# A two-layer transformer with routed experts on one Trainium2 core: the first expert blocks straight behind the choice of experts

## The chip, the core and the metric

The kernel runs on one core of a Trainium2 chip. The metric is the device time of one execution in microseconds (us). The engines are PE (TensorE, matmuls; its weight loads are listed as PEld), DVE (VectorE), ACT (ScalarE), POOL (GpSimd) and SP (SyncE, which issues nearly all DMAs).

## The reference

A sequence of 256 tokens of width 1024 passes two layers. Layer 0 mixes with a gated MLP, layer 1 with causal attention; behind each mixer stands a mixture of experts, and all vectors are modulated by a conditioning vector `c` (`ada`). The part at issue is `moe`, computed once in each layer:

```python
scores = jax.nn.sigmoid((xt @ w_router).astype(jnp.float32))
choice = scores + e_bias
...
choice = jnp.where(emask, choice, NEG_INF)      # the best 4 of 8 groups
_, eidx = lax.top_k(choice, TOP_K)              # 8 of 64 experts for each token
w = jnp.take_along_axis(scores, eidx, axis=1)
w = w / jnp.sum(w, axis=-1, keepdims=True) * ROUTED_SCALE
routed = grouped_experts(xt, eidx, w, w_gate, w_up, w_down)
shared = swiglu(xt, ws_gate, ws_up, ws_down)
return (routed + shared)
```

Each expert is `(silu(x @ wg) * (x @ wu)) @ wd` with 1024 x 256, 1024 x 256 and 256 x 1024 weights in float32, so 3 MB; all 64 are read in each layer, 192 MB. The shared expert has the same size and takes all tokens.

## The kernel before, in words

**Weights.** Every weight comes in loads of 1 MB (`load`, L255), issued by SP in one fixed order into 14 buffers ("w" tiles): 9 of a pool for the whole program and 5 of the stage's own. An expert is three loads, written here as e.0 (gate and up, first half of the contraction), e.1 (second half) and e.2 (down). A load is issued when the tile that used its buffer before has been read for the last time; SP waits there, and all later loads wait behind it.

**The stage of experts** (`moe`, L669) does this in each layer. Experts 0 and 1 and the shared expert are loaded before anything is known of the tokens. The router's logits are made, the scores (`sc`), the choice, and from the counts the rank of every expert: PE, DVE and PE again end in the tile `order` (L845), from which SP reads the number of each further expert before it loads it (`get_w`, L905). So expert weights beyond 0 and 1 cannot be asked for earlier than `order`. Ranks, not expert numbers, have a fixed number of token slots (`CAPS`); `_plan` (L70) cuts the slots, in the order of the list `ORDER`, into 55 blocks of 64, b0 to b54: one expert with 64 slots, or two with 32 each. `_loads` (L115) plans in the same order which buffer pool each load takes.

**Between the choice and b0** PE and DVE work through what the code writes there, each engine in the order of the program: sums of the conditioning vector that are still open (in layer 0, L852, 16 matmuls `wk<-w,cs`; in layer 1 the second gate is finished by `flush` in L889), the shared expert's gate and up product (`shared_up`, L769: 32 matmuls of 128x256, in pieces of 4, 12, 4 and 12, the 4 of `SH1` before the choice), the slots (`psu`, `slotU`), the weights of the slots (`wsel`, `GT`, `gu`), and the scaling of the gate into the shared expert's down weights (`gates`, L762). Then come the slots' one-hot matrix (`prep`, L920), 32 gather matmuls for the first four blocks (`gather`, L951) and the share of each slot (`share`, L932).

**A block** (`run`, L1085): `gate_up` (16 or 32 matmuls), `act` (ACT silu, DVE product with the slot's share), then `down` of the block before, the transposition of the new block, `place`, the scatter of the block before that, and one fourth of the gather for the next group of four blocks. The shared expert's `shared_down` (8 matmuls of 128x512) stands ahead of block `SHARED_AT`, b3. Its three buffers carry expert weights afterwards, as do those of the open sums. `e.0` and `e.1` are free when `gate_up` has read them, `e.2` when `down` has, which stands behind the next block's `gate_up`.

In the trace an fp32 matmul is recorded as two, so `x24` are 12 matmuls. All operations are recorded at line 200, so rows are told apart by tiles: `wk<-b,w 128*128` is `shared_up`, `wk<-w,b` `gate_up`, `wk<-w,ht` `down`, `acc<-w,s` `shared_down`, `wk<-s,b 128x256` the gather, `wk<-half,w` the end of an open sum.

Of the kernel before, what the change touches and what calls it, by code (L numbers as in the profile page):

```python
# [8 lines left out]
F32 = mybir.dt.float32  # L9
F32R = mybir.dt.float32r  # L10
# [6 lines left out]
P = 128  # L17
# [43 lines left out]

SH = -1
ORDER = [
# [3 lines left out]
]  # L67


# [34 lines left out]
BLOCKS, UNITS, SHARED_AT = _plan()  # L104


PAD = (224, 416)


SLOTS = 14  # L110
NOWN = 5
SH1 = 4


def _loads(l):  # L115

    last = {}
    for b, blk in enumerate(BLOCKS):  # L120
        for s in blk:
            if s:
                last[s[0]] = b
    items = [("e", k) for k in list(range(STATIC)) + [k for k in ORDER if k >= STATIC]]
    for i in reversed(range(NA if l == 0 else 0)):
        items.insert(AMONG[i][0], ("A", i, AMONG[i][1]))

    free = [(-9, 0)] * NOWN + [(-1, 1)] * 2 + [(2 * SHARED_AT - 1, 1)] + [(-2, 1)] * (SLOTS - NOWN - 3)
    own = []
    for x in items:  # L130
        for q in range(3 if x[0] == "e" else 1):
            free.sort()
            own.append(free[0][1] == 0)
            free[0] = (2 * last[x[1]] + (0 if q < 2 else 3) if x[0] == "e" else 2 * x[2] + 4, free[0][1])
    return items, own
# [50 lines left out]
def tile_model(ctx: ExitStack, tc: tile.TileContext, A: dict, out: bass.AP):  # L186
# [101 lines left out]
    def tb(name, rows=P):  # L288
        a, n = _TAB[name]
        return tab[0:rows, a:a + n]  # L290
# [25 lines left out]
    G.affine_select(tris, onesb[0:NE, 0:NE], [[1, NE]], ALU.is_gt, 0.0, base=0, channel_multiplier=-1)  # L316
    mhalf = cst.tile([P, 2], F32, name="mhalf")
    G.memset(mhalf, -0.5)
    pidxb = cst.tile([NE, 1], BF16, name="pidxb")
    G.iota(pidxb, [[0, 1]], base=0, channel_multiplier=1, allow_small_or_imprecise_dtypes=True)  # L320
    cs = cst.tile([P, KT], F32, name="cs")
# [347 lines left out]
    def moe(l, own, rw, first, rest):  # L669

        def om(shape, dt=F32, tag="sm", bufs=5):
            return own.tile(list(shape), dt, tag=tag, name=nm(tag), bufs=bufs)
# [54 lines left out]
        logits(4)  # L727
        pr = along([r[:, tt:tt + 1] for tt in range(2)])
        rb = h1((P, 256))
        S.copy(rb, pr)  # L730
        acc = accs()
        for q, x in enumerate(xs):
            T.matmul(acc[q], ident, x, start=True, stop=True, skip_group_check=True)
# [2 lines left out]
        lg = om([P, 2, NE])  # L736
        for tt in range(2):
            V.scalar_tensor_tensor(lg[:, tt, :], pl[tt], r[:, tt:tt + 1], cb, ALU.mult, ALU.add)
        for k, eng, b in ((0, V, pr), (4, G, rb)):
            eng.tensor_tensor(hT[:, k:k + 4, :], xT[:, k:k + 4, :], b.unsqueeze(1).to_broadcast([P, 4, 256]), ALU.mult)  # L740


        sc = om([P, 2, NE])
        S.activation(sc, lg, AF.Tanh, scale=0.5)
        for k in range(KT):
            S.activation(hT[:, k, :], hT[:, k, :], AF.Identity, bias=sh2[:, k:k + 1], scale=sc2[:, k:k + 1])
        for q in range(4):
# [1 line left out]
            t = s2((P, 512))  # L749
            S.activation(t, xs[q], AF.Copy, scale=r[:, q // 2:q // 2 + 1])  # L750
            G.tensor_tensor(pieces(rl)[q], t, pieces(rh)[q], ALU.subtract)
        V.tensor_scalar(sc, sc, 0.5, 0.5, ALU.mult, ALU.add)

        wsh = first[0]
        hid = s2((P, 2, 256))
# [6 lines left out]
        def gates():  # L762

            for q in range(2):
                S.copy(gq[64 * q:64 * q + 64, :], g2[l][64 * q:64 * q + 64, 512 * q:512 * q + 512])
            for k, eng in enumerate((G, V)):
                eng.tensor_tensor(wsh[2][:, k, :], wsh[2][:, k, :], g2[l], ALU.mult)

        def shared_up(n):  # L769
            for f, q, k in todo[:n]:  # L770
                if q == k == 0:
                    psh.append(wk((P, 2, 256)))
                T.matmul(psh[f][:, q, :], wsh[k // 4][:, k % 4, q * 256 + f * P:q * 256 + (f + 1) * P], hT[:, k, :],
                         start=(k == 0), stop=(k == KT - 1))
            del todo[:n]
# [50 lines left out]
            T.matmul(pn[:, 0:NE], c64b, sel[:, tt, :], start=(tt == 0), stop=(tt == 1))  # L826
        for tt in range(2):
            T.matmul(pn[:, NE:NE + 1], sel[:, tt, :], c64b[:, 0:1], start=(tt == 0), stop=(tt == 1))
        slot = om([P, 2, NE], BF16, tag="slot", bufs=1)
        V.tensor_tensor(slot, pc, sel, ALU.mult)  # L830
        keyr = om([NE, NE])
# [20 lines left out]
        while sums:  # L852
            rest(1)
            pump(T, S)
        shared_up(16 - SH1)
        slotT = om([NE, 256], BF16, tag="slotT", bufs=1)
        V.tensor_copy(slotT, pst)
        puf = om([NE, NU], tag="puf", bufs=1)
        V.tensor_scalar(puf, tb("rk", NE), rank, None, ALU.is_equal)
        pub = om([NE, NU], BF16, tag="pub", bufs=1)  # L860
        V.tensor_copy(pub, puf)

        wsel = om([P, 2, NE])
        wsum = om([P, 2], tag="t1", bufs=8)
        for tt in range(2):
            V.scalar_tensor_tensor(wsel[:, tt, :], cr[:, tt, :], -2.5e38, sc[:, tt, :], ALU.is_lt, ALU.mult,
                                   accum_out=wsum[:, tt:tt + 1])
        wrec = om([P, 2], tag="t1", bufs=8)
        V.reciprocal(wrec, wsum)
        for tt in range(2):  # L870
            V.tensor_scalar(wsel[:, tt, :], wsel[:, tt, :], wrec[:, tt:tt + 1], 2.5, ALU.mult, ALU.mult)
        ready = all(f.dst is None for f in active)
        if ready:
            gates()
        psu = wk((P, 2, NU))
        for tt in range(2):
            T.matmul(psu[:, tt, :], slotT[:, tt * P:(tt + 1) * P], pub, start=True, stop=True)
        settle(1)
        close()
        shared_up(4)  # L880
        pgt = wk((NE, 256))
        for tt in range(2):
            T.transpose(pgt[:, tt * P:(tt + 1) * P], wsel[:, tt, :], ident)
        settle()
        close()
        GT = om([NE, 256], tag="GT", bufs=1)
        S.copy(GT, pgt)
# [3 lines left out]
        pgu = wk((P, 2, NU))
        for tt in range(2):
            T.matmul(pgu[:, tt, :], GT[:, tt * P:(tt + 1) * P], puf, start=True, stop=True)
        gu = om([P, 2, NU, 2], F32R, tag="gu", bufs=1)
        V.tensor_copy(gu[:, :, :, 0], pgu)
        V.tensor_tensor(gu[:, :, :, 1], pgu, gu[:, :, :, 0], ALU.subtract)
        shared_up(12)
        slotU = om([P, 2, NU], tag="slotU", bufs=1)
        V.tensor_tensor(slotU, psu, tb("base").unsqueeze(1).to_broadcast([P, 2, NU]), ALU.subtract)

# [135 lines left out]

        ng = NU // 8
        prep(0)
        shared_act(0)
        shared_act(1)  # L1040
        for c in range(4):
            gather(0, c)
        share(0)
        prep(1)

        found = []

# [37 lines left out]
        def run():  # L1085
            ht, ys, sts, segs = {}, {}, {}, {}
            i0, _ = _TAB["idx"]

            def finish(b):

                return down(ht.pop(b), segs.pop(b))

            for b in range(nblk + 2):
                g, j = divmod(b, 4)

                late = b >= nblk - 1
                if b == SHARED_AT:
                    shared_down()
                if b == nblk - 1:
                    ys[b - 1] = halves(finish(b - 1))  # L1100
                if b < nblk:
                    segs[b] = segs_of(b)
                    hg = groups[g][3]
                    pg = gate_up(lambda k, a0, a1: hg[:, k, j * 64 + a0:j * 64 + a1], segs[b])
                    hd = act(pg, groups[g][2][64:128, j // 2, j % 2:j % 2 + 1])
                if late:
                    if b < nblk:
                        scatter(sts.pop(b - 2), ys.pop(b - 2))
                        ht[b] = flip(hd)
                        scatter(sts.pop(b - 1), ys.pop(b - 1))  # L1110
                    if b == nblk:
                        y = finish(b - 1)
                    if b == nblk + 1:
                        warm(10)
                        scatter(sts.pop(b - 2), ys.pop(b - 2))
                elif b:
                    y = finish(b - 1)
                if b < nblk:
                    if not late:
                        ht[b] = flip(hd)  # L1120
                    pp = place(groups[g][1][:, 2 * j:2 * j + 2, :].rearrange("e u i -> e (u i)"))
                    if b >= 2 and not late:
                        scatter(sts.pop(b - 2), ys.pop(b - 2))
                    if j == 1 and g + 1 < ng:
                        share(g + 1)
                    if g + 1 < ng:
                        gather(g + 1, j)
                if b == nblk or b >= 1 and not late:
                    ys[b - 1] = halves(y)
                if b < nblk:  # L1130
                    sts[b] = placed(pp, tab[:, i0 + b:i0 + b + 1])
                    if j == 3 and g + 2 < ng:
# [638 lines left out]
```

## Time and profile before

| | |
|---|---|
| median of 3 runs | 1399.44 us (1397.13 to 1403.96) |
| the profiled execution, its own time | 1401.17 us |
| its span, first to last instruction | 1399.4 us, mean granted clock of TensorE 0.978 |
| PE / DVE / ACT / POOL busy | 96% / 54% / 32% / 4% |
| read from HBM | 513.75 MB, 368 GB/s over the span |
| DMA queue of SP (q1) | 513.77 MB, 90.5% of 16 engines' span |
| PE waiting for expert weights (`PE wk <- DMA w<-in_wexp_dram`) | 20.2 us in 14 waits |

The span is the profiled execution between its first and its last instruction. The page's 40 slices (35 us each) show two long stretches in which the DMA engines are full at 425 or 426 GB/s: the expert stages, from slice 8 to 20 and from 28 to the end. PE is shown as busy for 96% of the span, but the ends of pipelined matmuls are modelled, so that a full PE row does not say that PE is what the program waits for.

### The profile page before, as it was taken

What the parts mean: (1) busy time and instruction counts of PE and PEld (TensorE: products, weight loads), DVE (VectorE), ACT (ScalarE), POOL (GpSimd) and SP (SyncE); (2) the same over time, 40 slices, a digit from 0 to 9 for tenths busy, and PEclk for the clock granted to TensorE, in tenths of its full rate; (3) what the DMA queues carried; (4) which work ended last, traced back from release to release, by engine and by line L of the source; (5) the groups of instructions that cost most, each with busy time, mean ns of one, the idle gap of its engine ahead of it and who ended that gap; (6) DMA issues with size and microseconds to landing.
All of it is one profiled execution on the core that took longest, in us unless ns stands there. A gap on an engine that the chain in (4) does not pass through costs nothing. (4 is left out here: it accounts for less than half of the span.)

```text
span 1399.4 us, 26932 instructions
## 1 busy us (share of the span) xinstructions
PE 1339.6 (96%) x10954; PEld 886.3 (63%) x10954; DVE 758.0 (54%) x1408; ACT 452.2 (32%) x921; POOL 57.6 (4%) x70
## 2 busy tenths in 40 slices
PE   8999999899999999998989999999999999999997
PEld 6899776555655555564649886765565556555553
DVE  3599945444455444444458866554444444444444
ACT  4444424122232222222344543322223222232222
POOL 1000002000000000000010320200000000000000
PEclk8899999999999999999999989999999999999999
DMA  9999876699999999999998855669999999999995
GB/s 387 332 342 360 313 267 240 262 402 425 426 426 425 426 373 426 426 426 426 426 408 318 295 205 216 271 230 394 418 426 426 426 426 425 426 426 426 426 426 218
DMA packets 91128, 516.60 MB, mean 369 GB/s; under 512 B 8308, under 2 KB 8436, under 8 KB 34934
## 3 DMA queue, kind: packets, MB, share of 16 engines
q1 hardware_dynamic: 90420, 513.77, 90.5%
q8 instruction: 88, 1.44, 0.4%
q10 hardware_dynamic: 580, 1.06, 0.2%
q14 instruction: 40, 0.33, 0.1%
HBM read 513.75 MB, written 1.05 MB: 368 GB/s over the span
## 5 line engine op out<-in xcount | busy, mean ns | idle before, releaser
L200 PE MATMUL wk<-w,b 128*32 128x256 f32 (+1 forms) x4928 | 415.6, 387 | 20.2 <-DMA w<-in_wexp_dram 20.2
L200 PEld LDWEIGHTS wk<-w,b 128*32 128x32 f32 (+1 forms) x4928 | 236.0, 123 | 166.2 <-DMA w<-in_wexp_dram 22.4
L200 DVE TENSOR_TENSOR s<-s,s 64x512 fp32r<-64x512 f32 x220 | 151.1, 687 | 123.5 <-ACT s L200 121.8
L200 PE MATMUL wk<-w,ht 128*32 128x512 f32 (+1 forms) x1232 | 211.5, 599 | 0.0
L200 ACT ACTIVATE b<-wk,adaT,sc 128x256 f32<-128x256 f32 x112 | 63.3, 565 | 285.6 <-DVE b L200 285.6
L200 DVE TENSOR_SCALAR b<-wk,sc,adaT 128x256 f32<-128x256 f32 x112 | 60.9, 544 | 156.0 <-PE wk L200 155.8
L200 PE MATMUL wk<-s,b 128*128 128x256 f32 (+2 forms) x1024 | 140.8, 287 | 0.0
L200 ACT CAST s<-s 64x512 fp32r<-64x512 f32 x220 | 134.3, 611 | 15.5 <-DVE s L200 12.8
L200 PEld LDWEIGHTS wk<-s,b 128*128 128x128 f32 (+1 forms) x1024 | 130.9, 187 | 10.3 <-issue 1.1
L200 PE MATMUL acc<-s,h 128*128 128x512 f32 x440 | 132.7, 423 | 0.4 <-DVEq L1147 0.4
L200 DVE TENSOR_TENSOR s<-wk,g 128x512 f32<-128x512 f32 x110 | 76.1, 692 | 89.2 <-PE wk L200 88.9
L200 PEld LDWEIGHTS wk<-w,ht 128*32 128x32 f32 (+1 forms) x1232 | 53.3, 121 | 99.7 <-issue 91.6
L200 ACT ACTIVATE h<-wk 64x256 f32<-64x256 f32 (+1 forms) x114 | 42.9, 376 | 211.7 <-PE wk L200 211.6
L200 DVE SCALAR_TENSOR_TENSOR h<-wk,ws,h 64x256 f32<-64x256 f32 x110 | 54.0, 491 | 98.1 <-ACT h L200 97.3
L200 DVE TENSOR_TENSOR scr<-w,scr 128x1024 fp32r<-128x1024 f32 x80 | 97.5, 1232 | 10.2 <-ACT scr L200 10.1
L200 ACT CAST scr<-w 128x1024 fp32r<-128x1024 f32 x80 | 83.1, 1047 | 51.7 <-PE wk L200 33.2
L200 PEld LDWEIGHTS acc<-s,h 128*128 128x128 f32 x440 | 74.4, 189 | 24.0 <-DVEq L1147 1.1
L200 ACT COPY ht<-wk 128x128 f32<-128x128 f32 x110 | 29.3, 266 | 185.4 <-PE wk L200 185.4
L200 PEld LDWEIGHTS wk<-ident,h 64*128 64x128 f32 (+1 forms) x226 | 22.5, 137 | 94.8 <-DVE h L200 93.9
L200 PE MATMUL wk<-hh,scr 128*128 128x256 f32 x576 | 73.0, 286 | 1.3 <-POOL hh L200 1.3
L200 PEld LDWEIGHTS wk<-hh,scr 128*128 128x128 f32 x576 | 70.5, 194 | 1.7 <-POOL hh L200 1.7
L200 PE MATMUL acc<-scr,hh 128*128 128x256 f32 x384 | 52.9, 299 | 4.8 <-DVE hh L200 4.5
(245 smaller groups left out, 1238.8 us busy)
## 6 DMA issues: line engine op xcount, KB each, us to landing
w<-in_wexp_dram SPq DMA_DIRECT2D x384, 1024.0 KB, 16.6
w<-in_wada_dram SPq DMA_DIRECT2D x48, 1024.0 KB, 7.6
w<-in_win_dram SPq DMA_DIRECT2D x16, 1024.0 KB, 7.5
w<-in_wqkvo_dram SPq DMA_DIRECT2D x16, 1024.0 KB, 7.8
w<-in_wkva_dram SPq DMA_DIRECT2D x8, 1024.0 KB, 6.8
w<-in_wout_dram SPq DMA_DIRECT2D x8, 1024.0 KB, 7.5
w<-in_wsh_dram SPq DMA_DIRECT2D x6, 1024.0 KB, 6.6
xt<-in_x_dram SPq DMA_DIRECT2D x1, 1024.0 KB, 6.4
```

What stands on the lines that cost most here:

```text
L200: r = f(*a, **k)
```

## The change

Nothing is added to or taken from what is computed. (1) `sc` is finished on ACT by a second activation, straight behind the tanh, in place of a DVE operation behind DVE's half of `hT`; the copy `rb` stands behind them, and POOL's half of `hT` is cut in two. (2) Before the choice 8 matmuls of `shared_up` are issued instead of 4, 2 more between the count and the rank, 6 behind the open sums; the other 16, the second half, move into the loop, behind the `act` of b3 (`UP_AT`). (3) `prep(0)` and the gather come directly behind `psu` and `slotU`; six matmuls whose result nobody reads (`warm(6)`) stand ahead of them. The weights of the slots are computed during the gather; `share(0)`, `prep(1)`, the gates and the end of the open sums move behind `gate_up` of b0. (4) `ORDER` changes, `shared_down` moves to b4, and the planned release of the shared expert's buffers follows. The number of blocks stays 55.

```diff
-    0, 63, 21, -1, 52, 56, 1, 32, 7, 46, 43, 36, 45, 6, 25, 23, 44, 15, 20, 26, 27, 30, 51, 8, 11, 50, 28, 41,
+    0, 63, 21, 52, 56, 43, -1, 59, 7, 46, 1, 36, 45, 25, 23, 44, 15, 20, 26, 27, 30, 51, 8, 11, 9, 50, 28, 41,
...
-SH1 = 4
+SH1 = 8
+
+UP_AT = 3
...
-    free = [(-9, 0)] * NOWN + [(-1, 1)] * 2 + [(2 * SHARED_AT - 1, 1)] + [(-2, 1)] * (SLOTS - NOWN - 3)
+    free = [(-9, 0)] * NOWN + [(2 * UP_AT - 1, 1)] * 2 + [(2 * SHARED_AT - 1, 1)] + [(-2, 1)] * (SLOTS - NOWN - 3)
...
-        S.copy(rb, pr)
...
-        for k, eng, b in ((0, V, pr), (4, G, rb)):
-            eng.tensor_tensor(hT[:, k:k + 4, :], xT[:, k:k + 4, :], b.unsqueeze(1).to_broadcast([P, 4, 256]), ALU.mult)
...
         S.activation(sc, lg, AF.Tanh, scale=0.5)
+        S.activation(sc, sc, AF.Identity, bias=phalf, scale=0.5)
+        S.copy(rb, pr)
+        for k, n, eng, b in ((0, 4, V, pr), (4, 2, G, rb), (6, 2, G, rb)):
+            eng.tensor_tensor(hT[:, k:k + n, :], xT[:, k:k + n, :], b.unsqueeze(1).to_broadcast([P, n, 256]), ALU.mult)
...
-        V.tensor_scalar(sc, sc, 0.5, 0.5, ALU.mult, ALU.add)
...
+        shared_up(2)
         slot = om([P, 2, NE], BF16, tag="slot", bufs=1)
...
-        shared_up(16 - SH1)
+        shared_up(16 - SH1 - 2)
...
-        V.tensor_copy(pub, puf)
+        V.tensor_scalar(pub, tb("rk", NE), rank, None, ALU.is_equal)
+        psu = wk((P, 2, NU))
+        for tt in range(2):
+            T.matmul(psu[:, tt, :], slotT[:, tt * P:(tt + 1) * P], pub, start=True, stop=True)
...
-        ready = all(f.dst is None for f in active)
-        if ready:
-            gates()
-        psu = wk((P, 2, NU))
-        for tt in range(2):
-            T.matmul(psu[:, tt, :], slotT[:, tt * P:(tt + 1) * P], pub, start=True, stop=True)
-        settle(1)
-        close()
-        shared_up(4)
-        pgt = wk((NE, 256))
...
-        if not ready:
-            flush(lambda f: f.dst is not None)
-            gates()
...
-        shared_up(12)
...
         prep(0)
+        warm(6)
+        wrec = om([P, 2], tag="t1", bufs=8)
...
         shared_act(0)
-        shared_act(1)
+        pgt = wk((NE, 256))
         for c in range(4):
             gather(0, c)
-        share(0)
-        prep(1)
+            if c == 1:
+                for tt in range(2):
+                    T.transpose(pgt[:, tt * P:(tt + 1) * P], wsel[:, tt, :], ident)
+                GT = om([NE, 256], tag="GT", bufs=1)
+                S.copy(GT, pgt)
+        pgu = wk((P, 2, NU))
...
+        def late_gates():
+            flush()
+            gates()
...
+                    if b == 0:
+                        share(0)
+                        prep(1)
                     hd = act(pg, groups[g][2][64:128, j // 2, j % 2:j % 2 + 1])
+                    if b == 0:
+                        late_gates()
+                    if b == UP_AT:
+                        shared_up(16)
+                        shared_act(1)
```

What stands on PE in layer 0 between `order` and the end of b0, before the change (`cs` marks the open sums, `pub` the slots, `half` the end of a sum, `sm` and `puf` the slots' weights, `s,b` the gather, `gu` the share, `w_1985` weights of expert 0):

```order
L200 MATMUL wk_2187<-w_345,cs 32x512 x4
L200 MATMUL wk_2115<-b_299_2080,w_335 128x256 x4
L200 MATMUL wk_2115<-b_299_2080,w_333 128x256 x4
...
L200 MATMUL wk_2235<-pub_2221,slotT_2217 128x112
L200 MATMUL wk_2238<-half_80,w_345 128x2 x4
L200 MATMUL wk_2244<-b_299_2080,w_333 128x256 x4
L200 MATMUL wk_2249<-ident,sm_2223 64x128 x2
L200 MATMUL wk_2254<-puf_2219,GT_2252 128x112 x2
...
L200 MATMUL wk_2285<-s_345_2274,b_279_1997 128x256
...
L200 MATMUL wk_2329<-gu_2257,s_345_2274 128x8 x4
L200 MATMUL wk_2346<-w_1985,b_347_2278 64x256 x8
L200 MATMUL wk_2366<-ident,h_362_2363 128x64 x2
```

The same place in the changed kernel:

```order
L202 MATMUL wk_2196<-w_347,cs 32x512 x4
L202 MATMUL wk_2118<-b_299_2081,w_335 128x256 x2
L202 MATMUL wk_2118<-b_299_2081,w_337 128x256 x4
...
L202 MATMUL wk_2224<-pub_2222,slotT_2220 128x112
L202 MATMUL wk_2238<-onesf,ident 128x128 x6
L202 MATMUL wk_2255<-s_337_2233,b_279_1999 128x256
...
L202 MATMUL wk_2254<-ident,sm_2227 64x128 x2
...
L202 MATMUL wk_2303<-puf_2249,GT_2279 128x112 x2
L202 MATMUL wk_2309<-w_1987,b_339_2237 64x256 x8
...
L202 MATMUL wk_2326<-gu_2306,s_337_2233 128x8 x4
L202 MATMUL wk_2346<-half_80,w_347 128x2 x4
L202 MATMUL wk_2356<-ident,h_360_2343 128x64 x2
```

Six matmuls of `shared_up` are left in front of the gather, the share and the end of the open sum stand behind `gate_up` of b0, and the slots' weights lie inside the gather.

On PE in layer 0 around b3 (`w_2613` and `w_2595` are first loads of an expert of b3, `w_337` and `w_339` the shared expert's down weights), before:

```order
L200 MATMUL wk_2574<-s_358_2341,b_280_1998 128x256
L200 LDWEIGHTS pidxb
L200 MATMUL wk_2593<-ohjb_2514,pidxb 1x96
L200 MATMUL acc_2072<-w_337,s_306_2113 128x512
...
L200 MATMUL wk_2634<-w_2613,b_347_2278 32x256
...
L200 MATMUL wk_2670<-w_2529,ht_2565 64x512 x4
L200 MATMUL wk_2677<-ident,h_423_2667 128x64 x2
```

and now:

```order
L202 MATMUL wk_2564<-s_357_2338,b_280_2000 128x256
L202 LDWEIGHTS pidxb
L202 MATMUL wk_2583<-ohjb_2504,pidxb 1x96
L202 MATMUL wk_2616<-w_2595,b_339_2237 32x256
...
L202 MATMUL wk_2652<-b_299_2081,w_335 128x256 x4
L202 MATMUL wk_2652<-b_299_2081,w_337 128x256 x4
...
L202 MATMUL wk_2672<-w_2519,ht_2555 64x512 x4
...
L202 MATMUL acc_2073<-w_339,s_306_2116 128x512
...
L202 MATMUL wk_2753<-w_2732,b_359_2342 32x256
```

The 16 late matmuls of `shared_up` stand between `gate_up` of b3 and `down` of b2, and `shared_down` ahead of b4's `gate_up` instead of b3's.

What each load waits for also moves, as the buffers are handed on in another order. In layer 0 the first loads behind the choice, in the names of ranks, were released like this before: 63.0 to 63.2 by the open sums, 21.0 by the end of the last open sum, 21.1 and 21.2 by the shared expert's gate and up weights, 52.0 and 52.1 by b1's `gate_up`. Now 21.0 waits for the end of that sum behind b0's `gate_up`, 21.1 and 21.2 for b1's `gate_up`; 52.2 for b2's `gate_up`, 56.1 for `down` behind it, 43.0 to 59.0 for b3's `gate_up`, 59.1 and 59.2 for the late half of `shared_up`, 7.0 for `shared_down`. In layer 1 four loads (63.0 to 21.0) find free buffers in both; then 21.1 waits for the end of the second gate's sum, 21.2 and 52.0 before for the shared expert's gate and up weights, now for b1's `gate_up`; now 56.0 and 56.1 wait for b2's, 43.1 to 59.1 for b3's, 59.2 and 7.0 for the late half of `shared_up`, 7.1 for `down` behind it and 7.2 for `shared_down`.

## Rows read from the trace of the kernel before

**Rows 1.** Busy time by stretch: us, engines (count), granted clock, DMA share, GB/s.

```profile
223.00:290.00 67.00, 62.78 (x467) 40.73 (x461) 28.63 (x69) 14.58 (x29) 3.63 (x3) 0.97 0.72 272
290.00:500.00 210.00, 207.60 (x1854) 120.81 (x1849) 101.47 (x192) 58.82 (x127) 0.00 (x0) 0.99 1.01 426
505.00:517.00 12.00, 12.00 (x113) 6.54 (x110) 5.54 (x10) 2.97 (x7) 0.00 (x0) 1.00 0.70 273
898.00:960.00 62.00, 58.70 (x408) 37.84 (x409) 25.90 (x64) 13.34 (x27) 5.67 (x3) 0.96 0.75 286
```

**Rows 2.** Order of time, PE, end of layer 0's experts: start, length, what [idle].

```profile
710.92 1.93 PE L200 MATMUL wk<-w,b 128*32 128x256 f32 x30 [0.54 <-DMA w<-in_wexp_dram]
```

**Rows 3.** Waits of PE, 287 to 718 and 959 to 1388: us, times, longest.

```profile
PE wk L200 <- DMA w<-in_wexp_dram: 11.1, 5, 3.9
...
PE wk L200 <- DMA w<-in_wexp_dram: 9.1, 9, 3.0
```

**Rows 4.** SP: loads 21.0, 21.1, 52.0 issued; then landing times, 222 to 262.

```profile
232.82 0.34 SPq L259 DMA_DIRECT2D w<-in_wexp_dram  x1
...
239.58 0.33 SPq L259 DMA_DIRECT2D w<-in_wexp_dram  x1
...
253.66 0.34 SPq L259 DMA_DIRECT2D w<-in_wexp_dram  x1
...
DMA to landing us min/median/max: 4.9/7.5/10.2
```

**Rows 5.** Order of time, PE, layer 0, from the choice to b4's `gate_up`.

```profile
215.57 1.89 PE L200 MATMUL wk<-b,w 128*128 128x256 f32 x8
219.22 0.22 PE L200 MATMUL wk<-sel,tri 128*128 128x64 bf16 x2 [1.76 <-DVE sel L200]
...
221.21 4.93 PE L200 MATMUL wk<-w,cs 128*32 128x512 f32 x32
226.07 5.45 PE L200 MATMUL wk<-b,w 128*128 128x256 f32 x24
...
231.65 1.05 PE L200 MATMUL wk<-half,w 128*128 128x2 f32 x8
...
245.38 3.67 PE L200 MATMUL wk<-w,b 128*64 128x256 f32 x32
...
251.69 3.66 PE L200 MATMUL wk<-w,b 128*32 128x256 f32 x64
...
259.39 3.67 PE L200 MATMUL wk<-w,b 128*64 128x256 f32 x32
...
271.91 7.13 PE L200 MATMUL acc<-w,s 128*128 128x512 f32 x16
...
287.00 3.67 PE L200 MATMUL wk<-w,b 128*64 128x256 f32 x32
```

**Rows 6.** Order of time, PE, layer 1: `shared_up`, b0, b2, `shared_down`, b4.

```profile
897.19 8.35 PE L200 MATMUL wk<-b,w 128*128 128x256 f32 x24
...
922.34 3.67 PE L200 MATMUL wk<-w,b 128*64 128x256 f32 x32
...
936.35 3.67 PE L200 MATMUL wk<-w,b 128*64 128x256 f32 x32
...
944.84 7.13 PE L200 MATMUL acc<-w,s 128*128 128x512 f32 x16
...
959.92 2.38 PE L200 MATMUL wk<-w,b 128*64 128x256 f32 x20
```

**Rows 7.** Busy time by stretch, two stretches behind the two choices.

```profile
220.44:223.85 3.41, 3.13 (x19) 0.94 (x23) 2.93 (x6) 2.50 (x5) 3.41 (x4) 0.50 0.04 7
896.28:903.11 6.83, 6.42 (x17) 5.02 (x18) 4.29 (x14) 2.65 (x5) 3.99 (x4) 0.50 0.62 224
```

**Rows 8.** Order of time, DVE, layer 0: `sc` finished; `prep(1)` beside b0.

```profile
213.88 1.35 DVE L200 TENSOR_SCALAR sm<-sm 128x128 f32<-128x128 f32 x1
...
246.38 0.69 DVE L200 TENSOR_TENSOR s<-slotU,tab 128x512 fp32r<-128x512 f32 x1
```

More of the change, by code (lines that the diff above doesn't have):

```diff
@@ L104 @@
 BLOCKS, UNITS, SHARED_AT = _plan()
-PAD = (224, 416)
+PAD = (192, 416)
 SLOTS = 14
 NOWN = 5
-SH1 = 4
+SH1 = 8
+UP_AT = 3
 def _loads(l):
@@ L318, in tile_model @@
     G.memset(mhalf, -0.5)
+    phalf = cst.tile([P, 1], F32, name="phalf")
+    G.memset(phalf, 0.5)
     pidxb = cst.tile([NE, 1], BF16, name="pidxb")
@@ L854, in moe @@
             pump(T, S)
-        shared_up(16 - SH1)
+        shared_up(16 - SH1 - 2)
         slotT = om([NE, 256], BF16, tag="slotT", bufs=1)
         V.tensor_copy(slotT, pst)
-        puf = om([NE, NU], tag="puf", bufs=1)
-        V.tensor_scalar(puf, tb("rk", NE), rank, None, ALU.is_equal)
         pub = om([NE, NU], BF16, tag="pub", bufs=1)
-        V.tensor_copy(pub, puf)
+        V.tensor_scalar(pub, tb("rk", NE), rank, None, ALU.is_equal)
+        psu = wk((P, 2, NU))
+        for tt in range(2):
+            T.matmul(psu[:, tt, :], slotT[:, tt * P:(tt + 1) * P], pub, start=True, stop=True)
         wsel = om([P, 2, NE])
@@ L867, in moe @@
                                    accum_out=wsum[:, tt:tt + 1])
-        wrec = om([P, 2], tag="t1", bufs=8)
-        V.reciprocal(wrec, wsum)
-        for tt in range(2):
-            V.tensor_scalar(wsel[:, tt, :], wsel[:, tt, :], wrec[:, tt:tt + 1], 2.5, ALU.mult, ALU.mult)
-        ready = all(f.dst is None for f in active)
-        if ready:
-            gates()
-        psu = wk((P, 2, NU))
-        for tt in range(2):
-            T.matmul(psu[:, tt, :], slotT[:, tt * P:(tt + 1) * P], pub, start=True, stop=True)
-        settle(1)
-        close()
-        shared_up(4)
-        pgt = wk((NE, 256))
[L882 to L887, printed above, removed]
-        if not ready:
-            flush(lambda f: f.dst is not None)
-            gates()
[L891 to L896, printed above, removed]
-        shared_up(12)
         slotU = om([P, 2, NU], tag="slotU", bufs=1)
@@ L1038, in moe @@
         prep(0)
+        warm(6)
+        wrec = om([P, 2], tag="t1", bufs=8)
+        V.reciprocal(wrec, wsum)
+        for tt in range(2):
+            V.tensor_scalar(wsel[:, tt, :], wsel[:, tt, :], wrec[:, tt:tt + 1], 2.5, ALU.mult, ALU.mult)
+        puf = om([NE, NU], tag="puf", bufs=1)
+        V.tensor_scalar(puf, tb("rk", NE), rank, None, ALU.is_equal)
         shared_act(0)
-        shared_act(1)
+        pgt = wk((NE, 256))
         for c in range(4):
             gather(0, c)
-        share(0)
-        prep(1)
+            if c == 1:
+                for tt in range(2):
+                    T.transpose(pgt[:, tt * P:(tt + 1) * P], wsel[:, tt, :], ident)
+                GT = om([NE, 256], tag="GT", bufs=1)
+                S.copy(GT, pgt)
+        pgu = wk((P, 2, NU))
+        for tt in range(2):
+            T.matmul(pgu[:, tt, :], GT[:, tt * P:(tt + 1) * P], puf, start=True, stop=True)
+        gu = om([P, 2, NU, 2], F32R, tag="gu", bufs=1)
+        V.tensor_copy(gu[:, :, :, 0], pgu)
+        V.tensor_tensor(gu[:, :, :, 1], pgu, gu[:, :, :, 0], ALU.subtract)
+        def late_gates():
+            flush()
+            gates()
         found = []
```

4 rows, old and new, of the table ORDER are left out of this document.

## The prediction, made before the change was run

> **What bounds the kernel now.** The first view was DMA traffic by stretch. From 290 to 500 us the transfers run at 426 GB/s with a share of 1.01: full. From 223 to 290, behind layer 0's choice, they move 272 GB/s, from 505 to 517 they fall to 273, and from 898 to 960, behind layer 1's choice, to 286 [rows 1]. A load of 1.049 MB takes 2.46 us at 426 GB/s. The time lost is 67 x (1 - 272/426) = 24.2 us, 12 x (1 - 273/426) = 4.3 us and 62 x (1 - 286/426) = 20.4 us. The second view was the order of time on PE: the last `gate_up` of layer 0 waits 0.54 us for its weights [rows 2], so a stage ends when its last load has landed, and a load brought forward shortens the program. The third was PE's waits for expert weights: 11.1 us in 5 waits behind b4 in layer 0, 9.1 us in 9 in layer 1 [rows 3]. PE has that much room before it bounds the stage itself. The fourth was SP's queue. A load that finds the queue empty lands 4.9 us after its issue, the minimum; others land 2.46 us after the one ahead of them. 21.0 goes out at 232.82, 21.1 at 239.58, 52.0 at 253.66 [rows 4]. On PE the open sum ended at 231.65 + 1.05 and b1's `gate_up` began at 251.69 [rows 5]: SP issues as buffers come free, and the time lost above is SP waiting for them. A first buffer (e.0) comes free 2.0 us after its `gate_up` starts (251.69 to 253.66), e.1 at its end (3.67 us), e.2 after the `down` behind the next `gate_up`.
>
> **The choice.** `order` comes just ahead of 221.2 in layer 0 [rows 5] and 897.2 in layer 1 [rows 6]. I leave both. Finishing `sc` on ACT takes an operation off DVE, but now 8 matmuls of `shared_up` precede the choice: four took 1.89 us from 215.57, eight end at 219.2 or so, and the rank began at 219.22. Matmuls would hold PE to there.
>
> **From the choice to b0.** Layer 0: b0's `gate_up` starts at 245.4, 24.2 us behind the choice [rows 5]. Of 28 matmuls of `shared_up` behind it 6 stay, so 22 leave, at 5.45/12 = 0.454 us each: 10.0 us. The end of the open sum leaves, 1.05 us. The six warming matmuls are new; an estimate by half the columns of a 128x256 is 0.23 us each, 1.4 us. Behind both choices the clock fell to 0.50, the 1.2 GHz level, just after PE's pauses in the choice (one of 1.76 us ahead of the rank) [rows 5, 7]. The four extra matmuls fill part of them; at the upper level the 4.93 us of open sums should be 3.6, another 1.3 us. Sum: -10.0 - 1.05 + 1.4 - 1.3 = -10.9, b0 at 234.5, 13.3 behind the choice. Layer 1 has no 3.6 us of open sums there: 13.3 - 3.6 = 9.7, b0 at 907.0 where it was 922.3, 15.3 earlier. Twelve matmuls that took 8.35 us at the low clock [rows 6] are part of this.
>
> The Trainium skill bears on the clock ("TensorE: Matmul & The Clock Gate", Part 1: The HAM clock gate): idleness lowers it to half and sustained work brings it back. The 0.50 here agrees with the first half. If filling the pauses does not suffice by that rule, the open sums keep 4.93 us and layer 1 loses up to 2.7 us as well, and the total gain below would be 9 instead of 13.
>
> **Blocks b0 to b4.** b0 to b1 was 6.3 us; with the share, `prep(1)` (0.69 us of DVE [rows 8]) and the end of the sum behind `gate_up` I take 8.3 (ends: 6.3, all hidden; 8.8, all on the path). b1 to b2 stays 7.7. From b2 to the end of what stands ahead of b3 is 271.91 - 259.39 = 12.5 in layer 0 [rows 5] and 944.84 - 936.35 = 8.5 in layer 1 [rows 6]. Behind b3's `gate_up` come 16 matmuls of `shared_up`, 7.3 us, the ordinary rest of a block, 7.7 + 0.4 - 3.7 = 4.4, and `shared_down`, 7.1: b4 starts 3.7 + 18.8 behind b3. PE's own work is only moved, so b4 is hardly earlier.
>
> **The walk of the loads.** Layer 0: 63.0 to 63.2 are ahead of it. 21.0 waits for the open sum, now behind b0's `gate_up`: issued 239.9, landed 244.8, seven later than before. b1 starts at 242.8 and frees 21.1 (landed 249.7) and 21.2 (252.2); 52.0 and 52.1 follow at once to 257.1. b2 at 250.5 frees 52.2 at 254.2, landed 259.5; three loads of 56 follow by 266.9. b3 is ready at 263.0 but waits for 56.0 and 56.1, to 264.6; its end frees 43.0 at about 268.3 or just before. The queue then runs full through 43.2 and 59.2 to 283.7. b4 starts at 287.1 (before 287.0), and `shared_down`, done then, frees its buffer for 7.0: issued 287.5, landed 292.4, the 19th load. Before, 272 x 67 / 1049 = 17.4 loads had been moved by 290. The same 19 then take to 290 + 1.6 x 2.46 = 293.9, and landing is some 2.4 us behind (4.9 less the 2.46 of the transfer), near 296. The gain is between 1.5 and 4 us; I take 3.
>
> Layer 1: four loads find free buffers as before. 21.1 goes out when b0 and the sum behind it are done, 913.5, landed 918.4. b1 at 915.3 frees 21.2 and 52.0 (922.2 and 924.6), the queue runs to 929.6 with 52.2; b2 at 923.0 frees the next, and loads arrive without a gap to 7.1 at 956.6. b3 waits some 3 us for its weights, from 931.5 to 934.6, and b4 starts at 957.1 (before 959.9). 7.2 waits for `shared_down`: issued 957.6, landed 962.5, the 21st. Before, 286 x 62 / 1049 = 16.9 loads were moved by 960; 21 took to 970.0, landed 972 or so. Gain 7.5 to 9.9; I take 8.
>
> **The dip at 505.** Loads there waited for buffers that blocks of large experts held. The new `ORDER` spreads these otherwise: gain between 0 and 4.3; a second dip may open elsewhere, so I take 2. In the rest the same bytes run at the same rate. PE's room, 11.1 us in layer 0 and 9.1 + 2.8 in layer 1, is larger than each gain, so the end of each stage follows its last load, and what follows layer 0 shifts as a whole.
>
> A second rule of the Trainium skill speaks against the move of `sc`: by "SBUF — State Buffer", section "SBUF: two separate sides", a DVE operation with two SBUF inputs and a GpSimd operation exclude each other for a whole instruction. The sum that makes `choice` reads two SBUF tiles and would now stand beside POOL's half of `hT`; each choice would come about 0.4 us later, and the total gain would be 12.2. The 1.35 us of [rows 8] for 128 elements beside POOL agrees with it.
>
> **Sum.** 3 + 8 + 2 = 13. The profiled execution took 1401.17 us (span 1399.4); 13 less is 1388.2. It lies 1.7 above the median of the runs shown, so against that median the forecast is **1386.4 us**.
>
> **Rivals.** (A) *The lead is not kept.* PE bounds the stages behind b4, since its work is the same and b4 starts at 287.1 against 287.0. Layer 0 gains nothing, layer 1 only its 2.8 us: 1396.7. For it: PE's busy share of 96%. Against it: 11.1 and 9.1 us of waits for weights [rows 3], which a PE that set the pace would not have. It decides if the later blocks' small waits are no real room. Chance 0.17, with the gains that are too small to tell.
>
> (B) *The upper ends hold:* 4, 9.9 and 4.3 us, 18.2 in all: 1381.2. It needs a dip removed whole. Inside the faster cases, about 0.1.
>
> (C) *Slower: the shared expert's buffers come back too late.* They were released about 20 us behind the choice, and will be at about 58 (their last readers stand behind b3 and ahead of b4). Had b0 not come forward, the whole walk would be 10.9 and 15.3 us later, turning gains of 3 and 8 into losses of about 8 and 7 (of 2 the dip may give back): 1399.4 + 13 = 1412. The place is what stands ahead of b0: if DVE's slot matrix or the transposed weights hold the gather, b0 is late. It decides if b0 comes forward by less than 8 of the 10.9 in layer 0 or less than 7 of the 15.3 in layer 1. Against it: 10.0 of the 10.9 us are matmuls whose removal is counted, whatever DVE does. Chance 0.08.
>
> (D) *The move of `sc` does nothing,* or the choice comes later by the matmuls ahead of it. The first is already in the sum; each us of the second costs a us per layer.
>
> **Chances.** An effect of 0.5%, 7 us, is about what a measurement of this kernel can tell from no change. The forecast and (B), with all gains above 7, have 0.75; (A) and lesser gains 0.17; (C) 0.08. The range: low end 1378, (B) with 3 us more out of the 2 x 2.0 that b0 to b1 gives if all is hidden; high end 1398, which takes in (A). (C) is left out, and a little on either side.
>
> **What would show it.** b0's `gate_up` 13.3 us behind the choice in layer 0 and 9.8 in layer 1; granted clock 1.0 behind both choices; the rates of the 67 and 62 us above 272 and 286; b3 waiting 1.5 and 3 us for weights; b4 at about 287 and 957; a short DMA gap ahead of 7.0 and 7.2; the last `gate_up` of each stage still waiting for its weights. It is wrong if b0 is later than 237 or 915, if DMA falls under 400 GB/s somewhere else behind b4, or if PE's waits for weights vanish and the last blocks run without any.

## The result and the profile after

The changed kernel took **1389.91 us** (median of 12 runs, 1384.74 to 1396.48), the kernel before, in the same rounds, 1400.55. The ratio is 0.9927, 95% interval 0.9908 to 0.9947: some 10 us faster, between 7.4 and 12.9. Forecast were 1386.4 us and a gain of 13.

The profiled execution of the change took 1395.34 us (span 1393.6), 5.4 above its median. Part of that lies where nothing was changed: from the last expert load of layer 0 to layer 1's choice it needed 186.2 us, the profile of before 183.4, and other runs below between 177.8 and 186.3. So I compare, beside the medians, the **stage** of each layer: from the choice (the matmul `wk<-pr,pidxb`, C from here on) to the landing of the last expert load.

| | before | change |
|---|---|---|
| layer 0: C, last landing, stage | 220.7, 713.3, 492.6 | 221.3, 713.2, 491.9 |
| layer 1: C, last landing, stage | 896.7, 1382.5, 485.8 | 899.3, 1376.7, 477.4 |

The stages give 0.7 and 8.4 us, 9.1 together. DMA traffic by stretch in the changed kernel, columns as in [rows 1]:

```profile
223.00:290.00 67.00, 62.70 (x451) 40.23 (x447) 28.69 (x72) 15.07 (x30) 4.21 (x3) 0.90 0.72 283
290.00:500.00 210.00, 209.66 (x1879) 123.31 (x1870) 100.06 (x189) 58.73 (x127) 0.00 (x0) 1.00 1.01 423
505.00:517.00 12.00, 11.76 (x110) 6.72 (x106) 4.88 (x9) 2.59 (x6) 0.00 (x0) 1.00 1.01 426
613.00:625.00 12.00, 12.00 (x120) 7.50 (x120) 4.60 (x9) 3.68 (x9) 0.00 (x0) 1.00 0.86 322
901.00:963.00 62.00, 59.25 (x467) 37.13 (x469) 29.03 (x70) 14.51 (x29) 5.31 (x3) 0.97 0.88 350
```

Behind layer 1's choice 350 GB/s stand for 286 [rows 1]. Behind layer 0's there are only 283 for 272, and the clock there is lower, 0.90 for 0.97. The dip at 505 is gone; another stands at 613. Both stages still end on a wait for weights, as in [rows 2]. In layer 1 it has become small: 0.55 us of PE's weight loads at 1374.3, where before PE itself waited 0.85 and 0.58. Layer 0's:

```profile
708.28 5.20 PE L202 MATMUL wk<-w,b 128*32 128x256 f32 x62 [2.74 <-DMA w<-in_wexp_dram]
```

The order of time on PE in layer 0, to be held against [rows 5]: open sums, b0, the end of the sum, then b1, b2, b3, the late half of `shared_up`, `shared_down`, b4.

```profile
221.63 3.64 PE L202 MATMUL wk<-w,cs 128*32 128x512 f32 x32
...
234.38 3.67 PE L202 MATMUL wk<-w,b 128*64 128x256 f32 x32
...
238.46 1.03 PE L202 MATMUL wk<-half,w 128*128 128x2 f32 x8
241.04 0.44 PE L202 MATMUL wk<-ident,h 64*128 64x64 f32 x2 [1.55 <-DVE h L202]
...
243.77 5.35 PE L202 MATMUL wk<-w,b 128*32 128x256 f32 x64
...
253.15 3.67 PE L202 MATMUL wk<-w,b 128*64 128x256 f32 x32
...
261.44 0.47 PE L202 MATMUL wk<-ident,h 64*128 64x64 f32 x2 [2.75 <-DVE h L202]
...
266.06 4.80 PE L202 MATMUL wk<-w,b 128*32 128x256 f32 x64
270.80 7.17 PE L202 MATMUL wk<-b,w 128*128 128x256 f32 x32
...
282.25 7.03 PE L202 MATMUL acc<-w,s 128*128 128x512 f32 x16
289.20 3.66 PE L202 MATMUL wk<-w,b 128*32 128x256 f32 x64
```

b0 is 11 us earlier than before. But b1's `gate_up` takes 5.35 us where it took 3.66, b3's 4.80: PE waited for DVE just ahead (1.55 and 2.75 us), and the granted clock from 241 to 249 is 0.61. When b4 starts, at 289.2, nothing is left of the lead over 287.0 [rows 5]. In layer 1 it is, measured from C: b4 at 60.3 instead of 63.2 [rows 6].

```profile
908.98 3.67 PE L202 MATMUL wk<-w,b 128*64 128x256 f32 x32
...
959.63 3.66 PE L202 MATMUL wk<-w,b 128*32 128x256 f32 x64
```

What SP waited for in the change between 223 and 300 (us in total, times, longest): buffers that PE reads, nothing else of size.

```profile
SPq L261 <- PE wk L202: 41.0, 11, 13.6
SPq L261 <- PE acc L202: 10.3, 1, 10.3
```

The 10.3 us are the wait of load 7.0 for `shared_down`.

### The profile page after: what moved, and what is told of

The parts are those of the page before. It is cut to its first block, busy times and chain, and to the rows that moved or that the text cites. A ratio compares the mean times of both kernels' runs of the same rounds, so it can differ in the third digit from the quotient of the medians.

```text
span 1393.6 us, 26993 instructions
## 1 busy us (share of the span) xinstructions
PE 1343.6 (96%) x10978; PEld 892.6 (64%) x10978; DVE 753.5 (54%) x1406; ACT 452.6 (32%) x923; POOL 58.1 (4%) x73
## 5 line engine op out<-in xcount | busy, mean ns | idle before, releaser
L202 ACT ACTIVATE b<-wk,adaT,sc 128x256 f32<-128x256 f32 x112 | 63.1, 564 | 289.2 <-DVE b L202 289.2
L202 PEld LDWEIGHTS wk<-s,b 128*128 128x128 f32 (+1 forms) x1024 | 131.6, 188 | 11.1 <-issue 1.8
L202 DVE TENSOR_TENSOR scr<-w,scr 128x1024 fp32r<-128x1024 f32 x80 | 97.5, 1231 | 10.4 <-ACT scr L202 10.3
```

The costliest lines, as they stand in the source:

```text
L202: r = f(*a, **k)
```

## The experiments

All medians stand beside runs of the kernel before on the same chip, but not all on one chip, so rows are compared by the ratio. The stages and rates are those of one profiled execution each. The table gives the stretch of 80 us behind each choice (GB/s; 10 GB/s there are 0.76 of a load of 1.049 MB), b4's start behind C, and the stage.

| run | median us | ratio to before (95%) | layer 0: GB/s, b4, stage | layer 1: GB/s, b4, stage |
|---|---|---|---|---|
| before | | | 285, 66.3, 492.6 | 310, 63.2, 485.8 |
| change | 1389.9 | 0.9927 (0.9908 to 0.9947) | 292, 67.9, 491.9 | 354, 60.3, 477.4 |
| order_only | 1402.7 | 1.0006 (0.9985 to 1.0027) | 285, 66.5, 493.3 | 321, 61.8, 482.4 |
| code_only | 1397.9 | 0.9976 (0.9953 to 1.0) | 274, 66.4, 495.3 | 344, 59.2, 480.7 |
| no_late_up | 1385.5 | 0.9887 (0.9853 to 0.992) | 325, 63.4, 486.2 | 363, 55.9, 474.8 |
| hole_b3 | 1398.0 | 0.9988 (0.9963 to 1.0013) | 293, 69.6, 491.4 | 345, 62.2, 478.4 |
| up_b1 | 1385.5 | 0.9907 (0.9872 to 0.9942) | 326, 62.7, 484.9 | 372, 55.4, 473.1 |
| prep_first | 1387.6 | 0.9913 (0.9882 to 0.9944) | 302, 66.0, 489.4 | 363, 58.8, 475.0 |
| sums_first | 1389.9 | 0.9933 (0.9903 to 0.9963) | 313, 64.0, 488.7 | 365, 58.2, 474.7 |
| no_warm | 1388.5 | 0.9913 (0.9882 to 0.9944) | 293, 67.6, 492.6 | 359, 59.4, 476.0 |
| sc_dve | 1386.9 | 0.9913 (0.9884 to 0.9942) | 292, 67.9, 492.6 | 357, 59.8, 475.7 |
| nl_all | 1380.7 | 0.9874 (0.9841 to 0.9907) | 337, 59.1, 484.1 | 366, 54.8, 474.1 |
| nl_sh8 | 1387.4 | 0.9899 (0.9866 to 0.9932) | 336, 58.2, 487.8 | 366, 52.9, 477.1 |
| up_all | 1380.5 | 0.9851 (0.9823 to 0.988) | 339, 59.7, 483.0 | 374, 55.1, 472.3 |

(b4 of nl_sh8 is the end of its wait for weights.) How far a stage differs by chance can be read from change, no_warm and sc_dve, whose loads move alike: 491.9 to 492.6 and 475.7 to 477.4. With one exception, nl_sh8, the stage's length follows the loads moved in those 80 us. In layer 0 from code_only to up_all it is 65 GB/s x 80 us / 1.049 MB = 5.0 loads more and 12.3 us less: 2.5 us for one load, its transfer time. All that the edits do to PE, DVE and the clock counts by what it does to this number.

### The two parts alone

**order_only**: the kernel before with the new list (with its -1 where `shared_down` stays ahead of b3).

```diff
-    0, 63, 21, -1, 52, 56, 1, 32, 7, 46, 43, 36, 45, 6, 25, 23, 44, ...
+    0, 63, 21, -1, 52, 56, 43, 59, 7, 46, 1, 36, 45, 25, 23, 44, 15, ...
```

> The kernel before with the new ORDER alone (shared_down stays ahead of b3). Theory W (the gain comes from the earlier first blocks, and the new order only moves the dip near 510 us elsewhere): the dip at 505 to 517 us goes, 3 to 5 us of lost DMA time appear later in layer 0, layer 1 as before; time within 3 us of before. Rival O (the order makes most of the gain): 6 to 10 us faster.

Nothing came of it in the time: 1.0006. The dip at 505 went, as expected, and came back at 560 and 620, some 5 us in all. In the profile layer 0's stage is 0.7 us longer, but layer 1's 3.4 shorter, which was not expected.

**code_only**: the changed kernel with the old list, -1 placed so that `shared_down` stays ahead of b4.

```diff
-    0, 63, 21, 52, 56, 43, -1, 59, 7, 46, 1, 36, 45, ...
+    0, 63, 21, 52, 56, -1, 1, 32, 7, 46, 43, 36, 45, ...
```

> The changed kernel with the old order of ranks, shared_down still ahead of b4. Theory W: b0 at the same place as in the change, layer 1's last load 7 to 8 us earlier behind its choice, layer 0 about 0, a dip of some 4 us stays in layer 0: 8 to 10 us faster than before. Rival O: under 4 us faster.

3.4 us by the ratio, where theory W wanted 8 to 10. That is in rival O's range, but order_only has ruled rival O out. By the ratio the parts alone give 0 and 3, together 10. By the stages this is so in layer 0 only: -0.7 and -2.7 us alone, 0.7 together. In layer 1 they add: 3.4 and 5.1 alone, 8.4 together. What is likely behind layer 0 stands in SP's queue of code_only. In 291 to 300 it waited once,

```profile
SPq L261 <- PE wk L202: 7.5, 1, 7.5
```

and then issued 46.2 and what follows:

```profile
299.43 0.87 SPq L261 DMA_DIRECT2D w<-in_wexp_dram  x2
```

In the old order b4 is the first half of rank 1, which reads on in b5, so b4 frees no buffer; b5 began at 297.43, and 2.0 us later the queue went on. That hole falls just behind the 14 us of shared work that PE now does between b3 and b4. The new order puts 43 and 59 there, whose block frees six. That this gap is the reason was read from the trace and not shown: no run changed rank 1's place alone.

### The late half of the shared expert

**no_late_up**: the second half of `shared_up` back ahead of the gather.

```diff
-        shared_up(16 - SH1 - 2)
+        shared_up(32 - SH1 - 2)
...
-                    if b == UP_AT:
-                        shared_up(16)
-                        shared_act(1)
```

> The change with the second half of the shared expert's gate and up product back ahead of the gather, its two buffers planned as free from there. Theory W: b0 7.3 us later in both layers (241.7 and 9.7 + 7.3 = 17.0 behind the choice), b4 within 1 us of the change; a part of layer 1's gain is lost: 2 to 6 us slower than the change. Rival R (only what stands ahead of b4 in all counts): as the change within 1 us.

Wrong on both sides: it is **faster** than the change, 1385.5, its stages shorter by 5.7 and 2.6 us. (The intervals of the two ratios just overlap; the stages differ by more than chance.) b0 is 7 us later, 20.0 behind C, and b4 yet 4.5 earlier. Two causes were possible: two buffers held until b3, or PE's 7.2 us between b3 and b4.

**hole_b3**: no_late_up with further PE work behind b3 that holds no buffer.

```diff
+                    if b == 3:
+                        warm(27)
```

> The run with the shared expert's second half ahead of the gather, and 27 further matmuls of 128x128 (7.2 us of PE work that releases nothing) behind b3's gate_up. Theory B (buffers): PE has some 10 us of room behind b4, so at most 3 us slower than without them, 1385 to 1389 us. Rival H (PE's time between b3 and b4): all that the change lost against the early half comes back and more, 5 us or more slower, 1390 to 1393 us.

The added work was meant to be 7.2 us and took 6.3:

```profile
275.23 6.29 PE L202 MATMUL wk<-onesf,ident 128*128 128x128 f32 x54
```

Rival H holds: 12.5 us slower than no_late_up by the medians, 14 by the ratios, 8.8 by the stages, as bad as the late half itself or worse. PE's waits for weights behind b4, 9.9 and 5.3 us in no_late_up, did not cover it: the blocks b3 and b4 release the buffers that an empty queue is waiting for, and b4 is 6 us later, so that the 80 us move 293 GB/s for 325 and 345 for 363.

**up_b1**: the late half behind b1 (`UP_AT = 1`), with prep(1) ahead of the share.

> The run with prep(1) ahead of the share, and the second half of the shared expert's product behind b1 instead of b3. Theory B (what the late half costs is that it holds two buffers until b3): the two buffers come free some 30 us behind the choice instead of 55, the 23rd load lands 2 to 4 us earlier behind the choice in layer 0, 1383 to 1386 us. Rival H (it costs because PE spends 7.2 us in the blocks that release buffers): b2 and b3 later by 7 us and their buffers too, time as with prep(1) alone or slower, 1387 to 1391 us.

The two buffers come free some 22 us earlier (the loads into them go out 31 and 33 us behind C instead of 53 and 55) and b4 starts some 3.3 us earlier in both layers than with the late half behind b3 (prep_first): 4.5 and 1.9 us off the stages. By the ratio alone it can't be told from prep_first; the stages speak for theory B here. But the PE work moved with the buffers, and hole_b3 had shown that such work alone costs as much as the late half did. So PE's time between b3 and b4 is shown as a cause; how much the held buffers add was not separated.

### PE's pauses and the clock

**prep_first**:

```diff
-                        share(0)
                         prep(1)
+                        share(0)
```

> The change with prep(1) written ahead of share(0) behind b0's gate_up, so that DVE makes the one-hot matrix while it waits for the share's matmuls. Theory P (PE's pause of 1.55 us behind b0, where it waits for DVE, lets the clock fall and makes b1 and b2 late): the pause falls under 0.6 us, the clock stays 1.0 behind b0 in layer 0, b1's gate_up takes 3.67 instead of 5.35 us, b2 starts near 250.5 instead of 253.15, b4 some 2 us earlier; 1 to 3 us less than the change in all. Rival Q (the loads wait for something else): b1 earlier, time as the change.

The pause behind b0 fell from 1.55 to 0.59 us and b4 came 1.9 and 1.5 us earlier, but the clock did not stay up. From b0's start to b2's it is 0.90, in the change 0.82, and b1's `gate_up` takes as long as there:

```profile
241.83 0.31 PE L202 MATMUL wk<-ident,h 64*128 64x64 f32 x2 [0.59 <-DVE h L202]
...
243.44 5.35 PE L202 MATMUL wk<-w,b 128*32 128x256 f32 x64
```

So the earlier matrix is worth something (stages shorter by 2.5 and 2.4 us), and theory P is wrong in that the clock stays up; in layer 1 it was 1.00 there in both runs, so there the gain is not the clock's. By the median the difference from the change is within the intervals.

**sums_first**: also the open sum's end ahead of the gather.

```diff
         prep(0)
-        warm(6)
+        settle()
+        warm(6 if l else 2)
...
+        close()
```

> The run with prep(1) ahead of the share, and in layer 0 the end of the open sum (8 matmuls of two columns, 1.03 us) moved back ahead of the gather, in the place of four of the six warming matmuls. Theory S (the clock fell in b1 because of those narrow matmuls behind b0, not because of the pause): b0 within 0.5 us of where it was behind the choice, clock 1.0 behind it, b1's gate_up 3.67 instead of 5.35 us; load 21.0 issued some 10 us earlier; stage of layer 0 2 to 4 us shorter than with prep(1) alone. Rival P (pauses alone): b1's gate_up still over 5 us.

b1's `gate_up` took 3.66 us here, behind a pause of 1.39. That would fit theory S, but up_all has the same matmuls up to there and took 4.81, and hole_b3 has the narrow matmuls behind b0 and took 3.66. Of the eight runs with them there the clock fell in seven, of the four without in one. What lets it fall behind b0 is **not settled**. Layer 0's stage is 0.7 us shorter than in prep_first, less than the 2 to 4 expected, and the time is the same.

**no_warm**: the change without `warm(6)`.

> The change without the six warming matmuls, so that PE waits there for DVE's slot matrix. If they only fill time that DVE needs: b0 at the same place behind the choice, clock still 1.0 in the gather, time as the change within 2 us (1388 to 1392). If they hold the clock: the gather and b0's gate_up at the lower clock (b0's over 5 us), 2 to 5 us slower. If they stand on the path: b0 1 us earlier in each layer, 1 to 2 us faster.

They only fill a wait. Without them PE waits 1.30 us for DVE's matrix, the gather's halves take 2.15 us as in the change, b0 starts 13.1 us behind C, and the time is the same.

```profile
231.73 2.15 PE L202 MATMUL wk<-s,b 128*128 128x256 f32 x16 [1.30 <-DVE s L202]
```

### The choice

**sc_dve**: the last step of `sc` back on DVE.

```diff
-        S.activation(sc, sc, AF.Identity, bias=phalf, scale=0.5)
...
+        V.tensor_scalar(sc, sc, 0.5, 0.5, ALU.mult, ALU.add)
```

> The change with the last step of sc back on DVE, behind its half of hT, all else kept. My forecast's term (PE's matmuls hold the rank there, so the move is worth nothing): the rank's matmul at the same distance behind the first shared_up matmul, 3.6 us, time as the change within 2 us. Rival (the choice is DVE's chain): the choice 1 to 1.4 us later in each layer, 2 to 3 us slower.

Worth nothing, as forecast. The rank's matmul stands 3.6 us behind the first `shared_up` matmul in both (215.64 to 219.21, 217.31 to 220.92). C is even 0.43 us *later* in the change: 5.65 us behind that matmul, here 5.22. The last step ahead of C is DVE's `pr`, which stands beside POOL's work on `rl`. In the change:

```profile
220.34 0.89 DVE L202 TENSOR_SCALAR pr<-tab,rank 64x64 bf16<-64x64 f32 x1
```

```profile
219.92 4.98 POOL L202 TENSOR_TENSOR b<-s,b 128x512 fp32r<-128x512 f32 x4 [4.00 <-ACT s L202]
```

POOL's four pieces take some 1.25 us each, so the first ends at 221.2, and `pr` at 221.23. Here it is 222.4 and 222.47:

```profile
222.05 0.42 DVE L202 TENSOR_SCALAR pr<-tab,rank 64x64 bf16<-64x64 f32 x1
```

```profile
221.15 2.52 POOL L202 TENSOR_TENSOR b<-s,b 128x512 fp32r<-128x512 f32 x2 [4.05 <-ACT s L202]
```

And before it was 220.6 and 220.66:

```profile
220.36 0.30 DVE L200 TENSOR_SCALAR pr<-tab,rank 64x64 bf16<-64x64 f32 x1
```

```profile
219.34 4.97 POOL L200 TENSOR_TENSOR b<-s,b 128x512 fp32r<-128x512 f32 x4 [4.19 <-ACT s L200]
```

In all 14 profiles, in both layers, `pr` ends 0.04 to 0.05 us behind POOL's first piece. So of its 0.89 and 0.42 us what exceeds the 0.30 is a wait, and what counts is when POOL begins: 4.28 us behind the first `shared_up` matmul in the change, 3.84 here, 3.77 before. POOL waits for ACT there, and in the change ACT has the second activation of `sc`, 0.40 us, ahead of it. No run moved POOL's work itself.

### A better version

**nl_all**: no_late_up, prep_first and sums_first, and DVE's side work of a block (`tick`, `overflow`) behind the next block's activation instead of ahead of it.

```diff
                     hd = act(pg, groups[g][2][64:128, j // 2, j % 2:j % 2 + 1])
+                    if 0 < b < nblk - 1:
+                        side(b - 1)
...
-                while due and due[0][0] <= b:
-                    begin(due.pop(0)[1])
-                tick(1.6, 0.9, 0.9)
-                next(over, None)
+                if b >= nblk - 2:
+                    side(b)
```

> All that the runs so far suggest: the second half ahead of the gather, prep(1) ahead of the share, the open sum's end ahead of the gather, and DVE's side work of a block (sums of the next conditioning, the overflow count) behind the next block's activation, so that PE's pause of 2.75 us behind b2 in layer 0 goes. If the gains add: b2's pause under 1 us, layer 0's stage 2 to 4 us shorter than with the early half alone, 1381 to 1384 us. If the loads are limited by the buffers alone: as with the early half, 1385 to 1387 us.

The gains add in part. The stages are 7.8 and 3.3 us shorter than in the change, 11.1 together; the parts alone gave 8.3 (no_late_up), 4.9 (prep_first) and 1.0 more (sums_first). The pause of 2.75 us behind b2 is gone, b2 to b3 takes 8.2 us instead of 11 in no_late_up, b4 starts 59.1 us behind the choice, and the clock stays at 1.00 from 223 to 290. 1380.7 us.

**nl_sh8**: the same with `shared_down` ahead of b8 (the -1 of the list moved).

> The run with all improvements, with shared_down ahead of b8 instead of b4. Theory H (what stands on PE between the choice and b4 or b5 delays the release of buffers while DMA has none, and behind that the DMA is full anyway): b4 7 us earlier, one buffer less until b8; 1 to 2 more loads moved in the first 80 us, layer 0's stage 2 to 4 us shorter, 1377 to 1380 us. Theory B (a buffer held is what counts): no gain or a loss, 1381 to 1384 us.

Neither loads nor time were won: 336 and 366 GB/s, as without it, and stages 3.7 and 3.0 us longer. Here b4 has caught up with its weights:

```profile
282.62 6.04 PE L198 MATMUL wk<-w,b 128*32 128x256 f32 x59 [5.31 <-DMA w<-in_wexp_dram]
```

Work moved from ahead of b4 leaves PE waiting there, and comes back at b8: `shared_down` stands at 317.49 to 324.5, SP waits 7.8 us for it, and from 320 to 340 DMA moves 335 GB/s, 4.3 us lost, where nl_all at the same distance behind C moves 425. So in layer 0 the exception is a hole behind the 80 us; in layer 1 the rates behind them account for some 2 of the 3.0 us.

**up_all**: as nl_all, with the late half behind b1.

> All improvements, but with the second half of the shared expert's product behind b1 instead of ahead of the gather. By the loads moved in the first 80 us: behind b1 alone they were 24.8 and 28.4 against 24.8 and 27.7 ahead of the gather, so the same in layer 0 and 1 to 2 us less in layer 1: 1378 to 1381 us, not to be told from the run with all improvements by its interval.

1380.46 us, ratio 0.9851 (0.9823 to 0.988), the shortest stages of all, 483.0 and 472.3. Between it and nl_all the runs do not decide; both beat the change.

## Why the prediction held, point by point

**The choice.** Right for the rank: 219.21 for 219.22, with DVE now waiting 1.1 us for PE. But C came 0.5 us later behind the first `shared_up` matmul (5.65 for 5.15), through `pr`, which I had not listed. From the rule of the Trainium skill ("SBUF — State Buffer", section "SBUF: two separate sides"), that a DVE operation with two SBUF inputs and a GpSimd operation shut each other out for a whole instruction, I had worked out 0.4 us through the sum that makes `choice`. The exclusion agrees with `pr`, which ends with POOL's piece in every run, but not with the place: that sum took 0.33 us at 214.46 in the change. It was held in sc_dve instead, 1.26 us beside POOL's `hT`. The 1.35 us of [rows 8] that I had held to agree with the rule is an operation with one SBUF tile as input, so it shows the wait and not the condition of two inputs.

```profile
215.99 1.26 DVE L202 TENSOR_TENSOR sm<-sm,eb 128x128 f32<-128x128 f32 x1
```

**b0.** Right: 234.38 for 234.5, 9.67 behind the choice in layer 1 for 9.7; the open sums took 3.64 us for 3.6, since the clock no longer fell in the choice. In none of the 24 choices of the changed kernel and its variants does it fall there; in all four of before and order_only it does. The forecast's other case, in which it still falls there and the gain is 9, did not come: what is missing of the 13 is missing further on. (The forecast counted from the first matmul behind the choice, 0.3 to 0.5 us behind C; by that count b0 is 9.3 behind it in layer 1, and the b4 and 7.2 of layer 1 below are 60.0 and 60.2.)

**b1 to b4.** The step that failed in layer 0. "b1 to b2 stays 7.7" was 9.4, and b0 to b1 9.4 for 8.3, both in part at the lower clock, which I had followed up to b0 and no further. b4 came at 289.2 for 287.1, and 7.0 went out at 289.40 for 287.5. b3 came so late, at 266.06 for 263.0, that it found its weights landed. The clock is not the whole of it: in no_warm and sc_dve it fell in b1 for a shorter time (`gate_up` 4.61 and 4.92 us), but there b3 waited for its weights, and b4 came at 67.6 and 67.9 behind C, as in the change. In sc_dve:

```profile
266.69 5.34 PE L202 MATMUL wk<-w,b 128*32 128x256 f32 x62 [1.92 <-DMA w<-in_wexp_dram]
```

No run kept the clock up from b0 to b4 with the late half behind b3, so how much of the 2 us is the clock's stays open. In layer 1, where the clock stayed up to b3, b0 to b1 was 8.4, b1 to b2 7.7, b4 60.3 behind C for 59.9, and 7.2 went out 60.5 behind it for 60.4.

**The loads.** Layer 1's stage gained 8.4 for 8. Layer 0 gained 0.7 for 3 + 2. Of that the first 80 us gave 7 GB/s, 0.5 of a load, 1.3 us. The term for the dip was wrong in sign: 4.3 us at 505 went, and about 2 at 555 to 565 and 3 at 613 to 625 came, as in order_only.

**The sum.** 9.1 in the stages for 13; the medians say 10.6, between 7.4 and 12.9 by the interval. So the forecast held by layer 1's 8. Of the 5 us forecast for layer 0, 0.7 came. That the time lies in the range says little: 1378 to 1398 takes in even (A)'s 1396.7.

**The rivals.** (A) is refuted in layer 1, which gained 8.4 where it had 2.8. No gain in layer 0 is what layer 0 showed, but not for its reason: PE did not set the pace of the whole stage, it set the release of buffers up to b4. The waits for weights that spoke against it, 10.9 and 5.7 us behind b4 in the change, lie later, where DMA is full:

```profile
PE wk L202 <- DMA w<-in_wexp_dram: 10.9, 6, 5.5
```

```profile
PE wk L202 <- DMA w<-in_wexp_dram: 5.7, 1, 5.7
```

(C), buffers too late, did not make the kernel slower. no_late_up shows that 8.3 us of the stages went to the late half, and hole_b3 that PE's time between b3 and b4 alone costs that much; what the held buffers add is not separated.

## What to carry to other kernels

Where a stream of loads is starved only for its first stretch, count the loads moved in that stretch: here each one was worth its 2.5 us at the end, 480 us later. Work put "out of the way" costs by what it stands ahead of: the same 7.2 us of matmuls were cheap ahead of the gather, where they free two buffers at once, and dear between the blocks that free six each. A wait of PE later in the stage is no room for work early in it. And a step taken off one engine can come back through others: `sc` on ACT made POOL later, and POOL's piece held DVE's `pr`.

## What I had not expected

Two edits worth 0 and 3 us alone gave 10 together; by the stages they add in layer 1 and not in layer 0, where the one makes a hole in the release of buffers that the other fills (as read from the trace). The clock behind b0 fell to half in most runs (b1's `gate_up` 4.0 to 5.35 us) and not in others with the same instructions up to there (no_late_up 4.68, hole_b3 3.66); pauses of 0.59 to 1.55 us went ahead of it, and no run separates them from the narrow matmuls there.

And the unchanged program between the stages moved single runs by as much as an edit: its length, 177.8 to 186.3 us, goes with its granted clock. In the change and in up_b1, busy time by stretch from the last landing of layer 0 to layer 1's choice, or a little less:

```profile
713.00:897.00 184.00, 177.01 (x1233) 147.24 (x1224) 133.94 (x228) 83.94 (x187) 32.83 (x36) 0.94 0.74 272
```

```profile
708.00:885.00 177.00, 170.18 (x1235) 141.61 (x1234) 136.14 (x235) 85.36 (x190) 33.78 (x37) 0.99 0.76 281
```
